# A two-layer decoder trunk on one core: layer normalisation at the mixer joints in two parts, a fourth raw weight buffer, and the first query weights split without a hold

## The chip, the cores and the metric

The kernel runs on one core of one Trainium2 chip. The metric is device time of one execution in microseconds. TensorE (PE in the profile, PEld its weight loads) multiplies, VectorE (DVE) and ScalarE (ACT) do the elementwise work, GpSimd (POOL) a little of it, and SyncE (SP) issues the transfers.

## What is computed

Two layers, each a token mixer, a layer norm, an expert mixer (PEER), a second layer norm and a gated add. Layer 0's mixer is a state-space block (SSD), layer 1's is causal attention (MoBA). 256 tokens, model width 1024, all in float32:

```python
for i in range(DEPTH):
    mix = ssd_mixer(...) if kind == 0 else moba_attention(...)
    x = layer_norm(alpha * x + mix, ln_mix_g[i], ln_mix_b[i])
    ffn = peer_ffn(x, peer_w_q[i], peer_sub_keys[i], peer_u[i], peer_v[i])
    x = layer_norm(alpha * x + ffn, ln_ffn_g[i], ln_ffn_b[i])
    gate = jax.nn.sigmoid((x @ ple_w_gate[i]).astype(jnp.float32)).astype(x.dtype)
    x = x + gate * (p[i] @ ple_w_proj[i])
```

`layer_norm` takes mean and variance of a token's 1024 values, scales by `rsqrt(var + eps)`, then by `g`, and adds `b`. `peer_ffn` makes queries `xb @ w_q`, scores them against keys, and sums over the chosen ones of 16384 experts (128 chunks `u` on the way in, 128 chunks `v` on the way out; this kernel multiplies with all of them and weights the rest with zero).

## The kernel before

**Weights come in chunks.** A chunk is a [128 x 1024] float32 tile of 512 KB. `chunk` takes one of three `raw` buffers, has SP load it, and `split` makes two halves of each value, in the type fp32r: ScalarE copies the rounded value (`hi`, L113), VectorE subtracts it from the raw one (`lo`, L114). Both go to a tile `hl`, of which there are four. `mm3` then does three matmuls for one float32 product (hi·hi, hi·lo, lo·hi; L138). A raw buffer is free again when `lo` is done. All loads are issued by SP in the order of the program, so a load that waits for a raw buffer holds what is behind it.

**The order on each engine** is not written out by hand: a scheduling layer places the instructions of all engines by its own estimates, and `after(marks)` (a hold) keeps an instruction from being placed ahead of the marked ones. A fourth buffer or another order in the code therefore moves instructions in other places too.

**The stages.** SSD of layer 0 (to about 224 us), then the expert mixer: queries and keys, 128 chunks `u`, 128 chunks `v`. In its tail (`TAIL = 5`) the last five experts are multiplied for the first token half of 128 alone, then for the second, so that the first half's norm can start. Among the last 26 experts before those stand seven chunks `w_pg` of the output gate, so that 33 chunks come where PE has the matmuls of 26. Each layer then ends with norm and gate; layer 1 begins with attention, and repeats the rest.

**The joint** between mixer and expert mixer is `end_mixer`: the last output products of both token halves (`tb` 0 and 1) into four PSUM accumulators `acc`, then `layer_norm` of half 0 with transposes (`turn`) of its result into `xT`, which all queries read; then products `project` of the per-layer input, which need no norm; then `layer_norm` of half 1 and its transposes. `layer_norm` consists of: two sums with the residual on VectorE (L175), two tiny operations (L178, L179), the square on ScalarE (L181), two products of the centred value (L184), the variance (L185), a power on GpSimd (L186), and two scalings (L189).

**The first query chunk** (`hc == 0`) has its `lo` subtracted by GpSimd (`lo_on`), and its split is held behind the square and the power of half 0.

Of the kernel before, what the change touches and what calls it, by code (L numbers as in the profile page):

```python
# [17 lines left out]
P = 128  # L18
T = 256
# [38 lines left out]
class Net:  # L58
# [50 lines left out]
    def raw(self):  # L109
        return self.stream.tile([P, 1024], F32, tag="raw", bufs=3, name=self.name("raw"))  # L110

    def split(self, hi, lo, src, lo_on=None):
        a = self.nc.scalar.copy(hi, src)  # L113
        b = (lo_on or self.nc.vector).tensor_tensor(lo, src, hi.bitcast(F32), op=OP.subtract)  # L114
        return a.ins, b.ins

    def chunk(self, src, w=1024, parts=1, hl=None, lo_on=None, after=()):
        raw = self.raw()
        if hl is None:
            hl = self.stream.tile([P, 2, 1024], F32R, tag="hl", bufs=4, name=self.name("hl"))  # L120
        n = w // parts
        for k in range(parts):
            r = slice(k * n, (k + 1) * n)
            dma = self.nc.sync.dma_start(raw[:, r], src[:, r])
            with self.after(after):
                hi, lo = self.split(hl[:, 0, r], hl[:, 1, r], raw[:, r], lo_on)
            self.pace.marks = (dma.ins, hi) if lo_on else (dma.ins, hi, lo)
        return hl
# [40 lines left out]

    def layer_norm(self, tb, acc, x, gb, junks, dump, pool, keep=None, turns=True):  # L170
        nc = self.nc
        sm = pool.tile([P, 6], F32, tag="ln_s", bufs=2, name=self.name("ln_s"))
        for h in range(2):
            v = x[:, tb, h * 512:(h + 1) * 512]
            nc.vector.scalar_tensor_tensor(v, v, ALPHA, acc[h], op0=OP.mult, op1=OP.add, accum_out=sm[:, h:h + 1])  # L175
        v = x[:, tb, :]
        mean, neg, var = sm[:, 2:3], sm[:, 3:4], sm[:, 4:5]
        nc.vector.tensor_scalar(neg, sm[:, 0:1], sm[:, 1:2], -1.0 / D, op0=OP.add, op1=OP.mult)  # L178
        nc.vector.tensor_scalar(mean, sm[:, 0:1], sm[:, 1:2], 1.0 / D, op0=OP.add, op1=OP.mult)  # L179
        junk = junks[:, tb]  # L180
# [25 lines left out]
    def end_mixer(self, i, accs, x, gb, dump, pool, last, lhs):  # L206
# [20 lines left out]
        self.norm_marks[1] = self.norm_marks[1][:2] + (last,)  # L227

# [429 lines left out]
    def peer(self, i):  # L658
        nc, dram = self.nc, self.dram
        with self.tc.tile_pool(name=f"peer{i}", bufs=1) as pool:  # L660
# [251 lines left out]
            self.layer_norm(1, accs[1], x, gb0, gb1, junk[:, 0, 0], pool, turns=False)  # L912

# [129 lines left out]
```

## Time and profile before

| what | value |
|---|---|
| median of 3 runs | 2028.8 us (2027.66 to 2029.06) |
| the profiled execution, its own time | 2027.79 us |
| its span, first to last instruction | 2026.0 us |
| PE busy / PEld busy | 2001.7 us (99%) / 1817.5 us (90%) |
| DVE / ACT / POOL busy | 1553.3 (77%) / 1010.6 (50%) / 26.4 us (1%) |
| read from HBM | 360.92 MB, 181 GB/s over the span |
| granted clock of TensorE | 1.000 over the span |

A busy share close to one does not say that PE is at its peak: matmuls overlap, and their ends are modelled. The count of matmuls in a stretch of given length says more, and so does what PE waited for. The queues in the profile are `q1 hardware_dynamic` (all loads) and two for instructions; there is none that GpSimd's software would feed.

### The profile page before, as it was taken

To read this page: it belongs to the slowest core of one execution; us is meant where nothing else is said; L and a number is where in the kernel's file an instruction comes from. 1 tells how busy PE (TensorE), PEld (TensorE's weight loads), DVE (VectorE), ACT (ScalarE), POOL (GpSimd) and SP (SyncE) were. 2 spreads that over 40 slices of the span, in tenths; PEclk is the share of its full clock that TensorE was granted. 3 is DMA by queue.
4 is the path that set the end of the run, shared out by engine and by line. 5 is a ranking of instruction groups with operands and counts; after the bars stand their busy time and mean duration, and the time that the engine had idled before them with its cause. 6 is when DMAs were issued, how large, how long until landed. Compare 5 with 4: busy or idle time off the path is not lost.

```text
span 2026.0 us, 36796 instructions
## 1 busy us (share of the span) xinstructions
PE 2001.7 (99%) x14706; PEld 1817.5 (90%) x14706; DVE 1553.3 (77%) x3050; ACT 1010.6 (50%) x1472; POOL 26.4 (1%) x31
## 2 busy tenths in 40 slices
PE   9999999999999999999999999999999999999998
PEld 8888899999999888888879889999999988888887
DVE  8786659997777988866665655999787888986665
ACT  6754544455444444445545654445544444445553
POOL 0001000000000000000000000000000000000000
PEclk9999999999999999999999999999999999999999
DMA  7446655555555555666745555555555555566672
GB/s 270 156 133 197 210 174 181 179 184 184 159 173 161 176 167 187 226 209 201 235 138 177 177 179 165 186 179 187 175 161 175 159 178 175 178 214 221 201 227 83
DMA packets 102732, 369.64 MB, mean 182 GB/s; under 512 B 11392, under 2 KB 12320, under 8 KB 100896
## 3 DMA queue, kind: packets, MB, share of 16 engines
q1 hardware_dynamic: 102560, 367.29, 56.1%
q8 instruction: 115, 1.88, 0.4%
q14 instruction: 57, 0.47, 0.1%
HBM read 360.92 MB, written 6.32 MB: 181 GB/s over the span
## 4 chain that ended last, share of the span: by engine, by line
PE 79%; issue 8%; DMA 5%; DVE 5%; ACT 2%; POOL 1%; SPq 0%; POOLq 0%; ACTq 0%
PE mm L138 42%; PE acc L138 31%; DMA raw<-in_v 3%; PE aux L830 3%; DVE hl L114 2%; ACT hl L113 1%; DVE cv_y L351 1%; DMA raw<-in_w_pg 1%; PE aux L689 1%; PE aux L456 0%; DMA raw<-in_w_xbc 0%; PE mm L166 0%; PE mm L371 0%; DMA raw<-in_w_q 0%; POOL sq L477 0%
## 5 line engine op out<-in xcount | busy, mean ns | idle before, releaser
L138 PE MATMUL mm<-xT,hl 128*128 128x256 f32 x8112 | 1003.4, 284 | 1.8 <-DVE hl L114 1.1
L138 PEld LDWEIGHTS mm<-xT,hl 128*128 128x128 f32 x8112 | 981.5, 192 | 6.3 <-issue 2.0
L114 DVE TENSOR_TENSOR hl<-raw,hl 128x1024 fp32r<-128x1024 f32 x624 | 758.6, 1221 | 282.3 <-ACT hl L113 280.2
L113 ACT CAST hl<-raw 128x1024 fp32r<-128x1024 f32 x626 | 654.8, 1047 | 291.6 <-PE mm L138 174.2
L138 PE MATMUL acc<-hl,w 128*128 128x512 f32 x3024 | 697.5, 391 | 1.5 <-DVE hl L114 0.7
L138 PEld LDWEIGHTS acc<-hl,w 128*128 128x128 f32 x3024 | 564.7, 188 | 120.7 <-DVE hl L114 2.3
L113 ACT CAST w<-act 128x256 fp32r<-128x256 f32 x252 | 101.9, 406 | 269.0 <-PE acc L138 261.1
L803 ACT ACTIVATE act<-mm 128x512 f32<-128x512 f32 x128 | 76.5, 598 | 227.6 <-PE mm L138 227.4
L114 DVE TENSOR_TENSOR w<-act,w 128x256 fp32r<-128x256 f32 x252 | 106.0, 421 | 43.7 <-ACT w L113 42.9
L837 DVE SCALAR_TENSOR_TENSOR act<-aux,act 128x256 f32<-128x256 f32 x256 | 90.5, 416 | 26.0 <-PE aux L830 26.0
L821 DVE TENSOR_TENSOR a<-oh,r 128x512 f16<-128x512 f16 x256 | 96.3, 417 | 0.0
L815 DVE TENSOR_TENSOR oh<-iota,r 128x1024 f16<-128x1024 f16 x128 | 87.2, 682 | 0.0
L830 PEld LDWEIGHTS <-oh 128*128 128x128 f16 x2048 | 63.3, 98 | 9.7 <-issue 8.4
L830 PE MATMUL aux<-a,oh 128*128 128x64 f16 x2048 | 70.9, 193 | 0.0
L817 DVE TENSOR_TENSOR oh<-iota,r 128x512 f16<-128x512 f16 x128 | 53.3, 417 | 0.0
L138 PE MATMUL acc<-hl,nhl 128*128 128x512 f32 x192 | 49.2, 407 | 0.0
L138 PEld LDWEIGHTS acc<-hl,nhl 128*128 128x128 f32 x192 | 34.8, 188 | 9.8 <-issue 1.0
L138 PE MATMUL acc<-act,xT 128*128 128x512 f32 (+1 forms) x186 | 40.8, 373 | 0.0
L138 PEld LDWEIGHTS acc<-act,xT 128*128 128x128 f32 x186 | 32.2, 189 | 5.6
L351 DVE SCALAR_TENSOR_TENSOR cv_y<-cv_raw,params,cv_y 128x253 f32<-128x253 f32 (+2 forms) x72 | 34.4, 486 | 2.3 <-ACT cv_y L348 1.8
L727 DVE MAX8 act<-act 128x8 f32<-128x128 f32 (+1 forms) x96 | 32.1, 334 | 2.3
L114 DVE TENSOR_TENSOR act<-raw,act 128x1024 fp32r<-128x1024 f32 x16 | 19.6, 1226 | 16.3 <-ACT act L113 16.2
(213 smaller groups left out, 1048.7 us busy)
## 6 DMA issues: line engine op xcount, KB each, us to landing
raw<-in_u SPq DMA_DIRECT2D x256, 512.0 KB, 3.6
raw<-in_v SPq DMA_DIRECT2D x256, 512.0 KB, 4.3
raw<-in_w_q SPq DMA_DIRECT2D x32, 512.0 KB, 4.5
raw<-in_w_xbc SPq DMA_DIRECT2D x24, 512.0 KB, 3.7
raw<-in_w_z SPq DMA_DIRECT2D x16, 512.0 KB, 3.5
raw<-in_w_so SPq DMA_DIRECT2D x16, 512.0 KB, 4.4
raw<-in_w_pg SPq DMA_DIRECT2D x16, 512.0 KB, 4.5
raw<-in_w_qk SPq DMA_DIRECT2D x16, 512.0 KB, 3.9
```

The source lines that it names most:

```text
L113: a = self.nc.scalar.copy(hi, src)
L114: b = (lo_on or self.nc.vector).tensor_tensor(lo, src, hi.bitcast(F32), op=OP.subtract)
L138: self.nc.tensor.matmul(out, lhs(a), rhs(b), start=start and i == 0, stop=stop and i == 2)
L351: nc.vector.scalar_tensor_tensor(y[:, d:], raw[:, :T - d], w(k), y[:, d:], op0=OP.mult, op1=OP.add)
L689: nc.tensor.matmul(pss[:, tb], q[:, tb * P:(tb + 1) * P], keys[:, hc, :], start=True, stop=True)
L727: nc.vector.max(vals[:, 8:], src)
L803: nc.scalar.activation(act[e // 32][:, e % 32 - 1:e % 32 + 1, :], cur["ph"], AF.Gelu_apprx_tanh)
L815: nc.vector.tensor_tensor(pairs(oh2), every(self.iota, P), twins(i2T, P), op=OP.is_equal)
L817: nc.vector.tensor_tensor(pairs(oh1), every(self.iota[:, 64 * half:64 * half + 64], 64), twins(i1T, 64), op=OP.is_equal)
L821: nc.vector.tensor_tensor(pairs(a2[:, k]), pairs(oh1), twins(g2[:, k], 64), op=OP.mult)
L830: nc.tensor.matmul(pg[:, t, :], oh2[:, t], a2[:, k, t], start=k == 0, stop=k == 1)
L837: nc.vector.scalar_tensor_tensor(v, pg[:, :, 32 * a:32 * a + 32].rearrange("p t e -> p e t"), 2.0 ** -12, v, op0=OP.mult, op1=OP.mult)
```

## The change

1. `raw` has four buffers in place of three, and the program is built with `dynamic_dma_scratch_size=4096`.
2. `layer_norm` is cut into `ln_sums` (residual sums, the two tiny operations, the square) and `ln_scale` (the rest). `end_mixer` calls `ln_sums` for both halves, then `ln_scale` for half 0; `ln_scale` of half 1 stays where its `layer_norm` was. At the joint behind the expert mixer the two parts follow each other as before.
3. The first query chunk is split like all others: `hi` by ScalarE, `lo` by VectorE, with no hold.
4. `norm_marks` loses the power, which no hold needs any more.

```diff
     def raw(self):
-        return self.stream.tile([P, 1024], F32, tag="raw", bufs=3, name=self.name("raw"))
+        return self.stream.tile([P, 1024], F32, tag="raw", bufs=4, name=self.name("raw"))
...
-    def split(self, hi, lo, src, lo_on=None):
+    def split(self, hi, lo, src):
         a = self.nc.scalar.copy(hi, src)
-        b = (lo_on or self.nc.vector).tensor_tensor(lo, src, hi.bitcast(F32), op=OP.subtract)
+        b = self.nc.vector.tensor_tensor(lo, src, hi.bitcast(F32), op=OP.subtract)
...
-    def layer_norm(self, tb, acc, x, gb, junks, dump, pool, keep=None, turns=True):
+    def ln_sums(self, tb, acc, x, dump, pool):
         nc = self.nc
         sm = pool.tile([P, 6], F32, tag="ln_s", bufs=2, name=self.name("ln_s"))
         for h in range(2):
             v = x[:, tb, h * 512:(h + 1) * 512]
             nc.vector.scalar_tensor_tensor(v, v, ALPHA, acc[h], op0=OP.mult, op1=OP.add, accum_out=sm[:, h:h + 1])
-        v = x[:, tb, :]
         mean, neg, var = sm[:, 2:3], sm[:, 3:4], sm[:, 4:5]
         nc.vector.tensor_scalar(neg, sm[:, 0:1], sm[:, 1:2], -1.0 / D, op0=OP.add, op1=OP.mult)
         nc.vector.tensor_scalar(mean, sm[:, 0:1], sm[:, 1:2], 1.0 / D, op0=OP.add, op1=OP.mult)
+        square = nc.scalar.activation(dump, x[:, tb, :], AF.Square, bias=neg, accum_out=var).ins
+        return mean, var, square
+
+    def ln_scale(self, tb, sums, x, gb, junks, keep=None, turns=True):
+        nc = self.nc
+        mean, var, square = sums
         junk = junks[:, tb]
-        square = nc.scalar.activation(dump, v, AF.Square, bias=neg, accum_out=var).ins
...
-        power = nc.gpsimd.tensor_tensor(var, var, self.mhalf[:, :1], op=OP.pow).ins
+        nc.gpsimd.tensor_tensor(var, var, self.mhalf[:, :1], op=OP.pow)
...
-        self.layer_norm(0, accs[0], x, gb, junks, dump, pool, self.x_d[i])
+        sums = [self.ln_sums(tb, accs[tb], x, dump, pool) for tb in range(2)]
+        self.ln_scale(0, sums[0], x, gb, junks, self.x_d[i])
...
-        self.layer_norm(1, accs[1], x, gb, junks, dump, pool, self.x_d[i], turns=False)
+        self.ln_scale(1, sums[1], x, gb, junks, self.x_d[i], turns=False)
...
-                marks = (sq0, pow0) if hc == 0 else (sq0, last) if hc < 2 else (sq1, last) if hc < 4 else ()
-                lo_on = nc.gpsimd if hc == 0 else None
-                self.stationary(pq[:, :T], self.chunk(dram["w_q"][i, hc], lo_on=lo_on, after=marks))
+                marks = () if hc == 0 else (sq0, last) if hc < 2 else (sq1, last) if hc < 4 else ()
+                self.stationary(pq[:, :T], self.chunk(dram["w_q"][i, hc], after=marks))
...
-    nc = bacc.Bacc("TRN2", target_bir_lowering=False, num_devices=1)
+    nc = bacc.Bacc("TRN2", target_bir_lowering=False, num_devices=1, dynamic_dma_scratch_size=4096)
```

What the change does to the order on the engines is seen best at three places. The first is VectorE at the joint of layer 0. `ln_s_2289` are the statistics of half 0, `ln_s_2344` those of half 1 (`ln_s_2295` in the changed kernel), `hl_2390` is the first query chunk, `acc_921` and `acc_922` are half 1's accumulators. Before:

```order
L185 TENSOR_SCALAR ln_s_2289<-ln_s_2289 128x1
L189 SCALAR_TENSOR_TENSOR xn<-junks,ln_s_2289,gb 128x512 x2
L175 SCALAR_TENSOR_TENSOR xn,ln_s_2344<-xn,acc_921 128x512
L175 SCALAR_TENSOR_TENSOR xn,ln_s_2344<-xn,acc_922 128x512
L178 TENSOR_SCALAR ln_s_2344<-ln_s_2344 128x1
L179 TENSOR_SCALAR ln_s_2344<-ln_s_2344 128x1
L114 TENSOR_TENSOR xT<-mm_2300,xT 128x4x128
L114 TENSOR_TENSOR xT<-mm_2309,xT 128x4x128
```

and in the changed kernel, where lines from L176 on have other numbers (the scalings are L193):

```order
L189 TENSOR_SCALAR ln_s_2289<-ln_s_2289 128x1
L193 SCALAR_TENSOR_TENSOR xn<-junks,ln_s_2289,gb 128x512 x2
L114 TENSOR_TENSOR hl_2390<-raw_2389,hl_2390 128x1024
L175 SCALAR_TENSOR_TENSOR xn,ln_s_2295<-xn,acc_921 128x512
L175 SCALAR_TENSOR_TENSOR xn,ln_s_2295<-xn,acc_922 128x512
L114 TENSOR_TENSOR xT<-mm_2306,xT 128x4x128
L177 TENSOR_SCALAR ln_s_2295<-ln_s_2295 128x1
L178 TENSOR_SCALAR ln_s_2295<-ln_s_2295 128x1
```

The sums of half 1 have stayed behind the scalings of half 0, and the subtraction of the first query chunk, which GpSimd did, now stands between the two.

The second place is VectorE at the joint of layer 1 (half 0 is `ln_s_12787`, half 1 `ln_s_12842`, then `ln_s_12793`; `hl_12888` is the first query chunk, `at_12650` the last attention output). Before:

```order
L114 TENSOR_TENSOR at_12650<-aux_12713,at_12650 128x256
L175 SCALAR_TENSOR_TENSOR x,ln_s_12787<-x,acc_11789 128x512
L175 SCALAR_TENSOR_TENSOR x,ln_s_12787<-x,acc_11790 128x512
L178 TENSOR_SCALAR ln_s_12787<-ln_s_12787 128x1
L179 TENSOR_SCALAR ln_s_12787<-ln_s_12787 128x1
L175 SCALAR_TENSOR_TENSOR x,ln_s_12842<-x,acc_11791 128x512
L184 SCALAR_TENSOR_TENSOR junks<-x,ln_s_12787,gb 128x512 x2
L185 TENSOR_SCALAR ln_s_12787<-ln_s_12787 128x1
L175 SCALAR_TENSOR_TENSOR x,ln_s_12842<-x,acc_11792 128x512
L189 SCALAR_TENSOR_TENSOR x<-junks,ln_s_12787,gb 128x512 x2
L178 TENSOR_SCALAR ln_s_12842<-ln_s_12842 128x1
L179 TENSOR_SCALAR ln_s_12842<-ln_s_12842 128x1
```

and in the changed kernel:

```order
L114 TENSOR_TENSOR hl_12888<-raw_12887,hl_12888 128x1024
L114 TENSOR_TENSOR at_12650<-aux_12713,at_12650 128x256
...
L188 SCALAR_TENSOR_TENSOR junks<-x,ln_s_12787,gb 128x512
L175 SCALAR_TENSOR_TENSOR x,ln_s_12793<-x,acc_11791 128x512
L188 SCALAR_TENSOR_TENSOR junks<-x,ln_s_12787,gb 128x512
L175 SCALAR_TENSOR_TENSOR x,ln_s_12793<-x,acc_11792 128x512
L189 TENSOR_SCALAR ln_s_12787<-ln_s_12787 128x1
L177 TENSOR_SCALAR ln_s_12793<-ln_s_12793 128x1
L178 TENSOR_SCALAR ln_s_12793<-ln_s_12793 128x1
L193 SCALAR_TENSOR_TENSOR x<-junks,ln_s_12787,gb 128x512 x2
```

Here the statistics of half 1 have moved ahead of the scalings of half 0, the variance of half 0 has moved behind the last sum of half 1, and the query chunk's subtraction stands ahead of the whole joint.

The third place is TensorE in the SSD stage, where z chunks are multiplied in plain float32 (`mm_671` to `mm_794`, each from a raw buffer of its own), `aux_759` and `aux_764` are small products of the scan, and `aux_811` needs a copy by ScalarE. Before:

```order
L138 MATMUL mm_623<-xT,hl_619 128x256 x24
L416 MATMUL aux_759<-cf_126,bf_125 128x128 x2
L427 MATMUL aux_764<-ident,xs_127 128x128 x4
L371 MATMUL mm_671<-xT_78,raw_672 128x256 x8
L371 MATMUL mm_691<-xT_78,raw_692 128x256 x8
...
L138 MATMUL mm_818<-xT,hl_820 128x256 x11
L441 MATMUL aux_811<-xe_771,bn_809 128x512
L138 MATMUL mm_818<-xT,hl_820 128x256 x13
```

and in the changed kernel:

```order
L138 MATMUL mm_623<-xT,hl_619 128x256 x24
L379 MATMUL mm_671<-xT_78,raw_672 128x256 x8
L424 MATMUL aux_759<-cf_126,bf_125 128x128 x2
L379 MATMUL mm_691<-xT_78,raw_692 128x256 x8
...
L138 MATMUL mm_818<-xT,hl_820 128x256 x22
L449 MATMUL aux_811<-xe_771,bn_809 128x512
L138 MATMUL mm_818<-xT,hl_820 128x256 x2
```

The first plain z product has moved ahead of the scan's products, and on SP its load ahead of the four 1 MB loads of `ac`; `aux_811` has moved 11 matmuls back. Between the joints, in the expert mixers, the order on TensorE is the same in both kernels, and on SP, ScalarE and VectorE only a few neighbours are exchanged.

## Rows read from the trace of the kernel before

**Rows 1.** The page, busy time of each engine with share and count.

```profile
PE 2001.7 (99%) x14706; PEld 1817.5 (90%) x14706; DVE 1553.3 (77%) x3050; ACT 1010.6 (50%) x1472; POOL 26.4 (1%) x31
```

**Rows 2.** Windows: us, busy PE, PEld, DVE, ACT, POOL (count), PEclk, DMA share, GB/s.

```profile
0.00:50.00 50.00, 45.15 (x328) 40.39 (x329) 40.75 (x106) 34.64 (x63) 0.20 (x4) 1.00 0.77 273
900.00:945.00 45.00, 45.00 (x200) 37.25 (x200) 27.35 (x34) 22.31 (x34) 0.00 (x0) 1.00 0.61 194
1000.00:1024.00 24.00, 22.42 (x94) 17.06 (x93) 15.29 (x18) 12.63 (x17) 0.00 (x0) 1.00 0.81 237
1930.00:1960.00 30.00, 29.30 (x128) 23.67 (x127) 18.54 (x22) 16.98 (x24) 0.00 (x0) 1.00 0.72 225
1960.00:1990.00 30.00, 28.38 (x120) 21.84 (x119) 19.43 (x24) 15.44 (x22) 0.00 (x0) 1.00 0.72 227
```

**Rows 3.** Groups by line, 1905 to 1990: busy us, mean ns, idle before, releaser.

```profile
L114 DVE TENSOR_TENSOR hl<-raw,hl 128x1024 fp32r<-128x1024 f32 x29 | 35.5, 1224 | 20.6 <-ACT hl L113 20.6
L113 ACT CAST hl<-raw 128x1024 fp32r<-128x1024 f32 x28 | 29.4, 1050 | 22.9 <-DMA raw<-in_v 22.8
```

**Rows 4.** DMA issues from 1910 to 1987: count, KB each, median us to landing.

```profile
raw<-in_v SPq DMA_DIRECT2D x26, 512.0 KB, 4.4
raw<-in_w_pg SPq DMA_DIRECT2D x7, 512.0 KB, 4.6
```

**Rows 5.** The scalings' line by tile: ns min/median/max, first and last start, forms.

```profile
L189 DVE SCALAR_TENSOR_TENSOR xn<-junks,ln_s,gb x4: 744/750/2861, 212.4 to 221.4; 128x512 f32<-128x512 f32 x4
```

**Rows 6.** Timeline of the joint of layer 0 and the queries behind it.

```profile
212.38 3.53 DVE L189 SCALAR_TENSOR_TENSOR xn<-junks,ln_s,gb 128x512 f32<-128x512 f32 x2 [0.66 <-POOL ln_s L186]
212.44 2.93 POOL L114 TENSOR_TENSOR hl<-raw,hl 128x1024 fp32r<-128x1024 f32 x1
215.83 0.68 DVE L175 SCALAR_TENSOR_TENSOR xn<-xn,acc 128x512 f32<-128x512 f32 x1
215.97 0.66 PE L166 MATMUL mm<-ident,xn 128*128 128x128 f32 x4 [1.52 <-DVE xn L189]
221.64 0.63 PE L166 MATMUL mm<-ident,xn 128*128 128x128 f32 x4 [0.89 <-DVE xn L189]
223.85 11.91 PE L138 MATMUL mm<-xT,hl 128*128 128x256 f32 x96
240.03 1.22 PE L138 MATMUL mm<-xT,hl 128*128 128x256 f32 x8 [0.26 <-DVE hl L114]
```

**Rows 7.** Timeline of the joint of layer 1.

```profile
1178.70 3.51 DVE L189 SCALAR_TENSOR_TENSOR x<-junks,ln_s,gb 128x512 f32<-128x512 f32 x2
1181.60 1.31 PE L166 MATMUL mm<-ident,x 128*128 128x128 f32 x8 [1.84 <-DVE x L189]
1182.13 0.20 DVE L178 TENSOR_SCALAR ln_s<-ln_s 128x1 f32<-128x1 f32 x1
1183.91 1.16 ACT L181 ACTIVATE dump<-x,ln_s 128x1024 f32<-128x1024 f32 x1
1186.90 1.29 PE L166 MATMUL mm<-ident,x 128*128 128x128 f32 x8 [0.99 <-DVE x L189]
1188.93 11.29 PE L138 MATMUL mm<-xT,hl 128*128 128x256 f32 x92 [0.74 <-DVE xT L114]
```

**Rows 8.** Waits of PE from 9 to 205: us in total, times, longest.

```profile
PE aux L495 <- DVE dg L489: 2.5, 2, 1.6
PE mm L138 <- DVE hl L114: 0.8, 2, 0.6
PE mm L371 <- DMA raw<-in_w_z: 0.5, 1, 0.5
```

**Rows 9.** Timeline of the SSD stage: TensorE's plain z products.

```profile
48.64 7.14 PE L371 MATMUL mm<-xT,raw 128*128 128x256 f32 x32 [0.45 <-DMA raw<-in_w_z]
```

**Rows 10.** Groups by line, whole span: the exponentials of the SSD stage.

```profile
L402 ACT ACTIVATE ac<-ac 128x2048 f32<-128x2048 f32 x4 | 7.6, 1904 | 0.0
L401 ACT ACTIVATE ce<-ce 128x1024 f32<-128x1024 f32 x4 | 4.2, 1050 | 0.0
```

More of the change, by code (lines that the diff above doesn't have):

```diff
@@ L109, in raw, with chunk @@
     def raw(self):
-        return self.stream.tile([P, 1024], F32, tag="raw", bufs=3, name=self.name("raw"))
-    def split(self, hi, lo, src, lo_on=None):
+        return self.stream.tile([P, 1024], F32, tag="raw", bufs=4, name=self.name("raw"))
+    def split(self, hi, lo, src):
         a = self.nc.scalar.copy(hi, src)
-        b = (lo_on or self.nc.vector).tensor_tensor(lo, src, hi.bitcast(F32), op=OP.subtract)
+        b = self.nc.vector.tensor_tensor(lo, src, hi.bitcast(F32), op=OP.subtract)
         return a.ins, b.ins
-    def chunk(self, src, w=1024, parts=1, hl=None, lo_on=None, after=()):
+    def chunk(self, src, w=1024, parts=1, hl=None, after=()):
         raw = self.raw()
@@ L125, in chunk @@
             with self.after(after):
-                hi, lo = self.split(hl[:, 0, r], hl[:, 1, r], raw[:, r], lo_on)
-            self.pace.marks = (dma.ins, hi) if lo_on else (dma.ins, hi, lo)
+                hi, lo = self.split(hl[:, 0, r], hl[:, 1, r], raw[:, r])
+            self.pace.marks = (dma.ins, hi, lo)
         return hl
@@ L193, in layer_norm @@
                 nc.sync.dma_start(keep[:, tb, c], x[:, tb, c])
-        self.norm_marks[tb] = (square, power, last)
+        self.norm_marks[tb] = (square, last)
+    def layer_norm(self, tb, acc, x, gb, junks, dump, pool):
+        self.ln_scale(tb, self.ln_sums(tb, acc, x, dump, pool), x, gb, junks, turns=False)
     def ple_load(self, i, pool):
@@ L226, in end_mixer @@
         last = self.turn(x, 1, 1)
-        self.norm_marks[1] = self.norm_marks[1][:2] + (last,)
+        self.norm_marks[1] = self.norm_marks[1][:1] + (last,)
     def ssd(self):
@@ L520, in value_head @@
         acc = [self.acc() for _ in range(2)]
-        hls = [self.chunk(self.dram["w_v"][kp], after=self.norm_marks[1][::2]) for kp in range(4)]
+        hls = [self.chunk(self.dram["w_v"][kp], after=self.norm_marks[1]) for kp in range(4)]
         for kp in range(4):
@@ L673, in query @@
                 pq = self.mm()
-                (sq0, pow0, _), (sq1, _, last) = self.norm_marks[0], self.norm_marks[1]
-                marks = (sq0, pow0) if hc == 0 else (sq0, last) if hc < 2 else (sq1, last) if hc < 4 else ()
-                lo_on = nc.gpsimd if hc == 0 else None
-                self.stationary(pq[:, :T], self.chunk(dram["w_q"][i, hc], lo_on=lo_on, after=marks))
+                (sq0, _), (sq1, last) = self.norm_marks[0], self.norm_marks[1]
+                marks = () if hc == 0 else (sq0, last) if hc < 2 else (sq1, last) if hc < 4 else ()
+                self.stationary(pq[:, :T], self.chunk(dram["w_q"][i, hc], after=marks))
                 if hc < 4:
@@ L904, in peer @@
                 expert_out(e, w, hl, 0)
-            self.layer_norm(0, accs[0], x, gb0, gb1, junk[:, 0, 0], pool, turns=False)
+            self.layer_norm(0, accs[0], x, gb0, gb1, junk[:, 0, 0], pool)
             for n in ORDER[12 - TAIL:]:
-                pgw[divmod(n, 4)] = self.chunk(dram["w_pg"][i, n], after=(self.norm_marks[0][2],))
+                pgw[divmod(n, 4)] = self.chunk(dram["w_pg"][i, n], after=(self.norm_marks[0][1],))
             for e, w, hl in end:
@@ L911, in peer @@
                     self.turn(x, 0, TURNS.index(e))
[L912 removed]
+            self.layer_norm(1, accs[1], x, gb0, gb1, junk[:, 0, 0], pool)
             def project(pg, tb, h, kps, c=slice(0, 512)):
```

## The prediction

> **What bounds the kernel now.** I read the busy shares first, then counts of matmuls in windows, then PE's waits at the places that the order touches. PE is busy for 99% of the span [rows 1], so the question is where it does less than it could in its busy time. For the `v` chunks the window from 900 to 945 gives the measure: 200 matmuls in 45.00 us, 0.225 us each, 2.70 us for the 12 of an expert. In the last 24 us of layer 0's tail PE does 94, which are worth 94 × 0.225 = 21.15 us: 2.85 us are lost. In layer 1's tail 128 in 30 us are worth 28.8 and 120 are worth 27.0: 1.2 and 3.0 lost [rows 2]. The two tails together lose 7.05 us. The two joints lose what PE waits for `xT` there: 1.52 + 0.89 = 2.41 us in layer 0 [rows 6] and 1.84 + 0.99 + 0.74 = 3.57 us in layer 1 [rows 7]. The SSD stage has waits of 3.8 us in its three longest kinds [rows 8]. The granted clock is 1.00 (the level of 2.4 GHz) in each of these windows [rows 2], so it plays no part.
>
> What ends last in the tails is the raw buffer. ScalarE stands idle for 22.9 us ahead of the `hi` copies there, 22.8 of them until a load has landed, and VectorE for ScalarE [rows 3]. A raw buffer goes round in 4.45 us from issue to landing [rows 4] + 1.05 `hi` + 1.22 `lo` [rows 3] and some 0.1 between them = 6.8 us; three buffers give a chunk every 2.27 us. Measured are 33 chunks in the 77 us of that window, 2.33 us each [rows 4]. PE wants 33 chunks in the time of 26 experts, 26 × 2.70 / 33 = 2.13 us each. So the stock in the four `hl` runs down by 0.2 us a chunk, is empty near the end, and there PE waits, most of all when the last five experts are taken for half 0 alone, at 1.35 us a chunk.
>
> **The tails: −6.4 us.** Four buffers at 6.8 us give a chunk every 1.70 us. The DMA engines would then have to bring 524 KB in 2.13 us, 246 GB/s; the start of the kernel has 273 GB/s at a share of 0.77 [rows 2], which is a chunk in 1.92 us. Both are under 2.13, so the stock stays full to the last five. These want five chunks at 1.35 us: four lie ready or in raw buffers, and the fifth goes to a tile of its own and need not wait for an `hl`. I leave 0.6 us for what isn't smooth, and take 7.05 − 0.6 = 6.4. Upper end of the gain: all 7.05. Lower end: the DMA engines stop at the 237 GB/s that they have at the share of 0.81, the highest shown [rows 2], which is 2.21 us a chunk. The shortfall falls from 33 × 0.20 = 6.6 us to 33 × 0.08 = 2.6 us, against a stock that now covers 6.6 − 4.2 = 2.4 in layer 1; but the burst at the end then finds it empty. I put 3.5 there, half.
>
> The row says that there is room, since the engines' share is 0.72 when PE waits [rows 2]. The Trainium skill, "DMA: Bandwidth & Descriptors", section "Queues, rings and completion order", says that on each DMA engine the descriptors of a queue are taken in the order of its ring. By that a fourth load waits behind the other three, each takes longer to land, and more buffers in flight would bring nothing once the ring always holds work; the sum would then be without the 6.4. The share of 0.72 speaks against an always full ring, and I keep 6.4.
>
> **The joint of layer 0: −1.1 us.** A scaling takes 0.75 us, but one took 2.86 [rows 5]: the pair took 3.53 us beside GpSimd's subtraction of 2.93 us [rows 6]. Without that neighbour the pair takes 2 × 0.75 less their overlap, 1.41: 2.12 us gained. What GpSimd did, VectorE now does between the pair and half 1's sums, for 1.22 us [rows 3]. So these sums start 0.9 us earlier, and some 0.2 more, as in the new order half 0's accumulators end three matmuls sooner less one that has been put in front (2 × 0.225 = 0.45, of which I count half). From half 1's sums at 215.83 to the queries at 223.85 the chain is the same 8.0 us [rows 6], and PE's own work in front of half 1's transposes ends earlier than that chain. The wait of 1.52 for half 0 vanishes, that for half 1 takes part of its place. Bounds: nothing, if the subtraction on VectorE finds its chunk late, and 2.41, if no wait is left.
>
> **The joint of layer 1: −1.4 us.** Here too the pair falls from 3.51 [rows 7] to 1.41, 2.10 us. But the variance of half 0 now stands behind half 1's last sum (0.68, as in [rows 6]) and the two tiny operations (some 0.3), so the pair starts 1.0 us later and ends 1.1 earlier. Behind it the two tiny operations are gone, 0.3 more, and half 1's square, which ScalarE began at 1183.91 [rows 7], is done before it is wanted. All that follows moves by 1.4: queries at 1187.5 in place of 1188.93. The query chunk's subtraction stands where VectorE waits for attention's last output and costs nothing there; if its load were late, ScalarE's copy for it would hold the last attention copies behind it. Bounds: nothing, and 3.57.
>
> **The queries: −0.3 us.** One more `w_q` chunk is loaded ahead of the joint, which covers the wait of 0.26 at 240 [rows 6]. Bounds 0 and 0.6.
>
> **SSD: −1.2 us, the least certain.** The first plain z load goes ahead of the broadcast loads of `ac`, so the wait of 0.5 for it goes, and earlier raws should take half or more of the 0.8 for `hl` [rows 8]. The longest, 2.5 for `dg`, I leave as it is: its product has lost a cover of three matmuls (0.36 us) and the chain ahead of it one convolution step. The exponentials, which ScalarE does among the z copies, come a little later, behind one more 512 KB load (1.92 us at 273 GB/s). In the new order a z copy stands behind one pair of them (1.05 + 1.90 us [rows 10]), while PE takes 7.14 us for two z chunks [rows 9], 3.57 for each: it is the slower one, and covers this delay about once. Bounds: a gain of all 3.8 us, and a loss of 1.9.
>
> **Attention, the `u` stage and the even part of `v`: nothing.** Their order on PE is unchanged or nearly so, and in the `v` window no matmul is lost [rows 2]. Earlier loads find no wait there to remove; attention may move by 0.5 either way.
>
> **Sum.** 6.4 + 1.1 + 1.4 + 0.3 + 1.2 = 10.4 us. The profiled execution's own time is 2027.79 us, which gives 2017.4; it lies 1.0 below the median of the runs, and from that the sum is 2018.4. I take 2018.0 us.
>
> **The rivals.**
> - *The tails give nothing back.* Either the DMA engines are full, as by the ring rule above, or the fourth buffer waits for an `hl` and not for a load. For it: a share of 0.81 in the worst stretch. Against it: ScalarE waits for landings in all of the tail and for no `hl` [rows 3]. Time: 2018.0 + 6.4 = 2024.4.
> - *The joints give nothing back*, because half 1's chain, with the subtraction now on VectorE, ends as late as before. For it: 1.22 of the 2.12 us goes back at once. Against it: GpSimd's 2.93 on the same work. Time: 2018.0 + 2.5 = 2020.5.
> - *SSD's waits nearly all go*, since loads come earlier in all of it: 3.8 in place of 1.2, 2015.4.
> - *Slower.* ScalarE's exponentials come to stand in front of PE's z products: PSUM has two buffers for these, so a z copy that waits for a pair of exponentials holds PE. All four pairs are 4.2 + 7.6 = 11.8 us [rows 10]. Time: 2018.0 + 1.2 + 11.8 = 2031.0. It decides once the `ac` loads land later than about 3.57 − 2.95 = 0.6 us per chunk beyond what PE's own z work covers, over all four pairs. Against it: in this trace PE waits 0.5 us for the z load and for no exponential above that [rows 8].
>
> **How the numbers follow.** A measurement of this kernel tells about 0.2%, 4 us, from no change, so faster means under 2024.7 and slower over 2032.9. Chances: the forecast 0.63, no gain in the tails 0.15, none in the joints 0.12, SSD's waits gone 0.06, the exponentials 0.04. The forecast, the joints' and SSD's case are faster, and half of the tails' case, as it lies at the bound: 0.63 + 0.12 + 0.06 + 0.07 = 0.88. The rest of the tails' case and most of the exponentials' is the same; slower needs more than one of these and gets 0.03. The range: the terms' bounds reach from about 2011 (17.4 us of gain) to 2027 (1.6) when all go one way, which they won't; 2013.5 to 2024.0 leaves out more than half of the tails' case, the exponentials' and a little on the low side, together some 0.18.
>
> **What would show it.** In the changed trace, windows at the two tails' ends should hold matmuls at 0.225 us each with no loss over 0.5, and ScalarE should wait there less for landings, at more than 230 GB/s. Both scalings of half 0 should take 0.75 each, GpSimd should have no subtraction, and the queries should begin 1.1 and 1.4 us sooner after the last mixer product than now. Wrong it would be if loads take 6 us or more to land in the tails while chunks still come every 2.3, or if PE waits for a ScalarE copy in the z products.

## The result, and the profile after

The changed kernel takes 2012.58 us (median of 6 runs, 2012.11 to 2014.34) against 2028.23 (6 runs, 2026.55 to 2029.35): ratio 0.9924, 95% interval [0.9913, 0.9935]. It is faster, by 15.7 us where 10.4 were forecast, and lies 0.9 us below the range. A second comparison on another chip (below) gave 2012.74 against 2026.46, 13.7 us.

The profiled execution took 2012.46 us, its span is 2010.3. First the busy times of the page, to be read against [rows 1]:

```profile
PE 1994.8 (99%) x14706; PEld 1818.2 (90%) x14706; DVE 1554.8 (77%) x3052; ACT 1001.0 (50%) x1472; POOL 19.6 (1%) x29
```

PE has the same 14,706 matmuls as before. So the n-th matmul of one trace can be set against the n-th of the other, and the difference of their starts, taken where stages begin, gives what each stage is worth (n is taken at 199.1, 223.8, 245, 1040, 1172.5, 1188.9 and 2000 us of the kernel before; differences are rounded):

| stage | forecast | measured |
|---|---|---|
| SSD, to the last mixer products | −1.2 | −2.2 |
| joint of layer 0 | −1.1 | −1.9 |
| queries of layer 0 | −0.3 | −0.7 |
| tail of layer 0 / of layer 1 | −6.4 | −3.0 / −4.5 |
| attention | 0 | −0.7 |
| joint of layer 1 | −1.4 | −2.1 |
| behind the last matmul | 0 | −0.5 |
| sum | −10.4 | −15.7 |

In all other stages the shift is 0.0. Windows over the tails, as in [rows 2] (us, busy PE, PEld, DVE, ACT, POOL, PEclk, DMA share, GB/s):

```profile
995.00:1019.00 24.00, 24.00 (x108) 19.89 (x106) 16.08 (x25) 11.39 (x16) 0.00 (x0) 1.00 0.70 241
1920.00:1950.00 30.00, 30.00 (x134) 24.87 (x133) 21.29 (x25) 17.93 (x26) 0.00 (x0) 1.00 0.75 246
1950.00:1975.00 25.00, 25.00 (x112) 20.72 (x111) 16.35 (x19) 13.65 (x19) 0.00 (x0) 1.00 0.58 193
```

TensorE now does 134 matmuls in 30 us and 112 in 25, 0.224 and 0.223 us each: nothing is lost. Groups by line in the tail of layer 1, as in [rows 3], and the loads there, as in [rows 4]:

```profile
L114 DVE TENSOR_TENSOR hl<-raw,hl 128x1024 fp32r<-128x1024 f32 x29 | 35.5, 1225 | 11.3 <-ACT hl L113 11.1
L113 ACT CAST hl<-raw 128x1024 fp32r<-128x1024 f32 x29 | 30.4, 1049 | 0.0
```

```profile
raw<-in_v SPq DMA_DIRECT2D x26, 512.0 KB, 4.3
raw<-in_w_pg SPq DMA_DIRECT2D x7, 512.0 KB, 4.4
```

ScalarE's 22.9 us of idle time ahead of the `hi` copies are gone, at 246 GB/s, the rate that the forecast asked for, and a load takes no longer to land than with three buffers (4.3 and 4.4 us against 4.4 and 4.6).

The scalings by tile, as in [rows 5], and TensorE's timeline at the two joints, as in [rows 6, 7]:

```profile
L193 DVE SCALAR_TENSOR_TENSOR xn<-junks,ln_s,gb x4: 747/749/753, 209.2 to 217.2; 128x512 f32<-128x512 f32 x4
L193 DVE SCALAR_TENSOR_TENSOR x<-junks,ln_s,gb x4: 746/750/753, 1170.5 to 1176.0; 128x512 f32<-128x512 f32 x4
```

```profile
211.40 1.03 PE L166 MATMUL mm<-ident,xn 128*128 128x128 f32 x8
217.41 0.63 PE L166 MATMUL mm<-ident,xn 128*128 128x128 f32 x4 [0.65 <-DVE xn L193]
219.68 0.51 PE L138 MATMUL mm<-xT,hl 128*128 128x256 f32 x2 [0.28 <-DVE xT L114]
...
1163.67 4.92 PE L138 MATMUL acc<-hl,at 128*128 128x512 f32 x20
1171.32 0.66 PE L166 MATMUL mm<-ident,x 128*128 128x128 f32 x4 [0.20 <-DVE x L193]
1176.21 1.29 PE L166 MATMUL mm<-ident,x 128*128 128x128 f32 x8 [0.81 <-DVE x L193]
1178.23 1.93 PE L138 MATMUL mm<-xT,hl 128*128 128x256 f32 x14 [0.74 <-DVE xT L114]
```

No scaling is held up any more. Of the 2.41 us that TensorE waited at the joint of layer 0, 0.93 are left; of 3.57 in layer 1, 1.75. PE's waits in the SSD stage, as in [rows 8] (from 9 to 203 us):

```profile
PE mm L138 <- ACT hl L113: 1.2, 1, 1.2
PE aux L449 <- ACT bn L447: 1.1, 2, 0.6
PE mm L138 <- DVE hl L114: 0.8, 1, 0.8
PE aux L503 <- DVE dg L497: 0.8, 1, 0.8
```

The wait for `dg` has fallen from 2.5 to 0.8. The 1.2 and 0.8 for `hl`, at 10 and 11 us, cost only 0.3 net, as the products ahead of them end earlier; in a second profile of the same kernel (run 5) neither is there, so they belong to this execution. Why `dg` comes sooner is seen on VectorE, at the operation ahead of GpSimd's power (`rs`). Before, and then after, where an earlier wait stands in the same queue:

```profile
93.73 0.15 DVE L485 TENSOR_SCALAR rs<-aux 128x2 f32<-128x2 f32 x1
```

```profile
85.75 1.00 DVE L359 SCALAR_TENSOR_TENSOR cv_y<-cv_raw,params,cv_y 128x253 f32<-128x253 f32 x2 [1.97 <-ACT cv_y L356]
...
91.21 0.15 DVE L493 TENSOR_SCALAR rs<-aux 128x2 f32<-128x2 f32 x1
```

Its input is ready at about 91 in both, but in the kernel before VectorE comes to it 2.5 us later: subtractions of chunks that landed late stand ahead. In the changed kernel the chunks landed earlier and VectorE even waits for ScalarE at 85.75. The same subtractions stand ahead of `rs` in both orders; one convolution step (0.48 us) has moved behind it.

### The profile page after: what moved, and what is told of

Same layout as the page of the kernel before. It is cut to its first block, busy times and chain, and to the rows that moved or that the text cites. A ratio compares the mean times of both kernels' runs of the same rounds, so it can differ in the third digit from the quotient of the medians.

```text
span 2010.3 us, 36808 instructions
## 1 busy us (share of the span) xinstructions
PE 1994.8 (99%) x14706; PEld 1818.2 (90%) x14706; DVE 1554.8 (77%) x3052; ACT 1001.0 (50%) x1472; POOL 19.6 (1%) x29
## 4 chain that ended last, share of the span: by engine, by line
PE 95%; DVE 2%; ACT 2%; DMA 1%; issue 1%; POOL 0%; SPq 0%; ACTq 0%; POOLq 0%
PE mm L138 47%; PE acc L138 41%; PE aux L837 3%; PE aux L696 1%; PE aux L584 1%; ACT hl L113 1%; PE mm L379 1%; DMA raw<-in_w_xbc 1%; PE aux L464 0%; DVE hl L114 0%; PE mm L166 0%; PE aux L606 0%; DVE cv_y L359 0%; PE aux L465 0%; POOL sq L485 0%
## 5 line engine op out<-in xcount | busy, mean ns | idle before, releaser
L359 DVE SCALAR_TENSOR_TENSOR cv_y<-cv_raw,params,cv_y 128x255 f32<-128x255 f32 (+2 forms) x72 | 33.9, 477 | 5.4 <-ACT cv_y L356 5.1
L690 ACT COPY act<-mm 128x256 f32<-128x256 f32 x32 | 11.9, 372 | 51.3 <-PE mm L138 51.3
```

Of the source, the lines that this page charges most:

```text
L359: nc.vector.scalar_tensor_tensor(y[:, d:], raw[:, :T - d], w(k), y[:, d:], op0=OP.mult, op1=OP.add)
```

## The experiments

The shifts by stage for all runs, worked out like the table above (us against the profiled execution of the kernel before; attention and joint 1 together, here up to 1200 us, so with the first queries behind the joint; "tails" is layer 0 / layer 1), with the ratio of the timed runs:

| run | SSD | joint 0 | queries | tails | attention, joint 1 | end | sum | ratio, interval |
|---|---|---|---|---|---|---|---|---|
| changed, again | −2.6 | −1.9 | −0.7 | −3.0 / −4.5 | −2.8 | −0.5 | −16.0 | 0.9934 [0.992, 0.9947] |
| 1 fourth raw only | −2.0 | −1.0 | −0.6 | −3.0 / −4.5 | −0.1 | 0.0 | −11.2 | 0.9952 [0.9939, 0.9966] |
| 2 without it | 0.6 | −1.1 | −0.7 | −0.3 / −3.5 | −2.4 | −0.5 | −7.7 | 0.9985 [0.9976, 0.9994] |
| 3 query split only | 0.7 | −0.9 | −0.7 | 0.3 / −2.0 | −0.6 | −0.5 | −3.6 | 0.9986 [0.9977, 0.9995] |
| 4 norm split only | 3.1 | 0.4 | −0.5 | −0.1 / −1.7 | 0.8 | 0.0 | 2.0 | 1.0004 [0.9995, 1.0013] |
| 6 without query split | −1.9 | −1.0 | −0.6 | −3.0 / −4.5 | 0.0 | 0.0 | −11.0 | 0.9948 [0.9935, 0.9962] |
| 7 without norm split | −2.0 | −1.8 | −0.7 | −3.0 / −4.5 | −2.8 | −0.5 | −15.3 | 0.9937 [0.9924, 0.9951] |
| 8 five raw | 1.0 | −1.9 | −0.7 | −3.0 / −4.5 | −2.6 | −0.5 | −12.2 | 0.9948 [0.9934, 0.9962] |
| 9 three raw, five `hl` | 0.1 | −2.8 | −0.5 | −0.4 / 0.0 | −3.0 | −0.5 | −7.0 | 0.9977 [0.9967, 0.9986] |
| 10 GpSimd, no hold | −2.4 | −1.0 | −0.6 | −3.0 / −4.5 | −2.8 | 0.0 | −14.4 | 0.9937 [0.992, 0.9953] |
| 11 five `hl` | −2.5 | −2.7 | −0.1 | −3.0 / −4.5 | −2.6 | −0.5 | −16.0 | 0.993 [0.9914, 0.9947] |
| 12 half 1 first | −2.1 | −1.9 | −0.7 | −3.0 / −4.5 | −3.5 | −0.5 | −16.1 | 0.9928 [0.9911, 0.9944] |

**Run 1: the fourth buffer alone**, in the kernel before:

```diff
-        return self.stream.tile([P, 1024], F32, tag="raw", bufs=3, name=self.name("raw"))
+        return self.stream.tile([P, 1024], F32, tag="raw", bufs=4, name=self.name("raw"))
...
-    nc = bacc.Bacc("TRN2", target_bir_lowering=False, num_devices=1)
+    nc = bacc.Bacc("TRN2", target_bir_lowering=False, num_devices=1, dynamic_dma_scratch_size=4096)
```

> The kernel before with the fourth raw buffer (and the smaller scratch that makes room for it) and nothing else. First theory, each part of the change acts where its own wait stood: this one part takes all of the tails (3.0 us in layer 0, 4.5 in layer 1, read from the shift of the same matmul between the two traces), SSD's 2.2 and the 0.5 behind the last matmul; both joints stay, since GpSimd still subtracts beside the scalings (a scaling of 2.8 to 2.9 us in each). Sum 10.2, so 2017.5 to 2018.5 in place of 2028.2, ratio 0.995. Rival, the buffer also feeds the joints and the queries behind them with earlier chunks: the joints shrink by more than 1 us each here too, 2015 or less, ratio 0.9935 or less. Second rival, SSD's gain came with the other parts: 2020, ratio 0.996.

Measured 2016.57 against 2025.59. SSD and the tails are as the first theory has them, to 0.2 us; the wait for `dg` is 0.7. It is wrong on the 0.5 at the end, and the rival is right in part: joint 0 gains 1.0 here already. Attention gains 0.5 too, but the joint behind it gives 0.4 of that back: a scaling there still takes 2.9 us, TensorE waits 2.08 us for it, and just behind that wait its granted clock stands at 0.50, the level of 1.2 GHz, for 3.4 us.

**Run 2: the rest without the fourth buffer**, the changed kernel with `bufs=3`.

> The changed kernel with three raw buffers: the split norm and the first query weights without GpSimd and hold, no fourth buffer. First theory: the joints' 2.0 and 1.9 us are all here, the wait of 0.5 in the queries too, and the tails stay as they were before (7.5 us of lost time), SSD too: gain 4.4, so about 2023.8, ratio 0.998. Rival, the joints need the fourth buffer because the first query chunk's load now competes with the mixer's last chunks for raw buffers: gain under 2 us, 2026.5 or more, ratio over 0.999, with waits of TensorE for a chunk in the last mixer products.

2022.32 against 2025.59. The joints' gain stays, though in layer 0 it is 1.1 and not 2.0; SSD gains nothing, its `dg` wait is 2.5. The tails moved by 0.3 and 3.5 though nothing there had been changed: see the spread below.

**Run 3: the query split alone**, in the kernel before:

```diff
-                marks = (sq0, pow0) if hc == 0 else (sq0, last) if hc < 2 else (sq1, last) if hc < 4 else ()
-                lo_on = nc.gpsimd if hc == 0 else None
+                marks = () if hc == 0 else (sq0, last) if hc < 2 else (sq1, last) if hc < 4 else ()
+                lo_on = None
```

> The kernel before, with the first query chunk split by ScalarE and VectorE and without its hold, and nothing else: the norm is whole, three raw buffers. First theory: what made the joints long was GpSimd's subtraction beside VectorE's scalings. Without it no scaling takes over 1 us, and each joint gains 1 to 2 us: 2 to 4 in all, 2024.2 to 2026.2, ratio 0.9985. Rival, the order of the sums made the gain: scalings of 0.75 us, but TensorE waits for the transposes' input as long as before, and the time is within 1 us of before, ratio 0.9995 to 1.0005.

2023.35 against 2025.59, inside the first theory's 2 to 4 us. All scalings take 0.75; joint 0 gains 0.9, joint 1 2.1 up to the first query, of which 1.5 goes again in the queries behind it: there the granted clock stands at 0.50 for 3.4 us, and 16 matmuls take 3.37 us that take 1.90 in the kernel before.

**Run 4: the norm in two parts alone**, with GpSimd's subtraction and hold.

> The kernel before, with the norm of the joints cut in two parts (sums and square of both halves first), GpSimd's subtraction and hold kept, three raw buffers. First theory: beside GpSimd's subtraction one scaling in each joint still takes 2.8 to 2.9 us, and the earlier sums save only the two tiny operations and a square that is ready: 0 to 0.8 us in all, ratio 0.9997 to 1. Rival, the order makes the gain: 2 us or more, 2026.2 or less, ratio 0.999 or less.

No gain can be told (1.0004), scalings of 2.8 us in both joints, and neither joint is shorter (+0.4, +0.8). The rival is out. The 3.1 in SSD is a 2.4 us wait for a z load (0.5 before) and, right behind it, a granted clock of 0.50 for 3.4 us, which costs another 1.6; the expectation had neither. The clock falls at joint 1 too, and this profiled execution is the slowest of the run's eleven, so the two joints' small losses are not to be put down to the norm.

**Run 5: the changed kernel again**, on the chip of runs 6 to 8.

> The changed kernel once more, beside the runs that follow, so that all stand against the same runs of the kernel before. The part with the fourth buffer alone gave 0.9952, the joints and queries alone 0.9985, together 0.9937 if they add up. First theory, they add up, and the first comparison's 0.9924 is a draw within its interval and the three-buffer kernel's own spread: 0.9930 to 0.9942, about 2013 where before takes 2025.6. Rival, they help each other (the joint gains more once its last chunks come early): 0.9926 or less.

2012.74 against 2026.46: 0.9934, where the first theory has it. The interval reaches down to the rival's 0.9926 as well, so that the parts add up is likely and not shown.

**Runs 6 and 7: without the query split, without the norm split.** Each takes one part of the changed kernel back.

> The changed kernel with the first query chunk as before: GpSimd subtracts, held behind square and power; four buffers and the norm in two parts stay. First theory, GpSimd's subtraction beside the scalings is what the joints lost: a scaling of 2.8 to 2.9 us comes back in both, TensorE waits 2 to 4 us more than in the changed kernel at the two joints, and the time is that of the fourth buffer alone, ratio 0.9945 to 0.9960. Rival, the norm in two parts carries the joints: within 1 us of the changed kernel.

> The changed kernel with the norm whole in each half (sums, square and scaling of half 0, then those of half 1); four buffers and the new query split stay. First theory, the two parts are worth little by themselves: 0 to 1 us slower than the changed kernel, all of it at the joint of layer 1, where the order differs most. Rival, they are half of the joints' gain: 1.5 to 2.5 us slower, with longer waits of TensorE for the transposes of half 1 in both layers.

2015.97 and 2014.09 against the changed kernel's 2012.74. In run 6 a scaling of 2.8 to 2.9 us is back in each joint, and they lose 0.9 and 2.8 us. Some 1 us of the 2.8 is the clock: it falls to 0.50 behind TensorE's wait of 2.29 us for that scaling, and the two executions with a mean granted clock of 0.999, the profiled one among them, took 2016.86 and 2017.0 us, the three with 1.000 took 2015.86 to 2015.97. In run 7 no stage differs from the changed kernel's first profile by more than its two profiles differ among themselves (0.4), and the joints by 0.1: in the traces the split of the norm is worth nothing. The medians are 1.35 us apart, which is less than the 1.6 to 1.8 us that the five executions of either kernel spread over. The scalings' line in run 6, and TensorE's stretches without and with work at joint 1 (columns as in [rows 2]):

```profile
L193 DVE SCALAR_TENSOR_TENSOR xn<-junks,ln_s,gb x4: 744/751/2879, 209.7 to 218.7; 128x512 f32<-128x512 f32 x4
L193 DVE SCALAR_TENSOR_TENSOR x<-junks,ln_s,gb x4: 741/748/2835, 1171.7 to 1179.2; 128x512 f32<-128x512 f32 x4
```

```profile
1172.30:1174.60 2.30, 0.05 (x1) 0.00 (x0) 2.30 (x2) 0.79 (x3) 1.74 (x1) 1.00 0.01 4
1175.80:1179.00 3.20, 3.20 (x10) 2.52 (x9) 2.54 (x6) 2.14 (x4) 0.54 (x1) 0.50 0.98 275
```

**Run 8: a fifth raw buffer**, `bufs=5`.

> The changed kernel with a fifth raw buffer. First theory, the tails are done: TensorE does 0.225 us a matmul there and ScalarE waits for TensorE, not for loads, so a fifth buffer gives nothing there, and elsewhere little: within 1 us of the changed kernel, with TensorE's tails the same to 0.1 us. Rival, SSD and attention, where the fourth gave 2.5 and 0.5, still wait for loads: 1.5 us or more sooner in SSD. Third, more loads in flight make the first ones land later (the first chunk landed at 8.87 in place of 8.58 with the fourth): the start loses another 0.3.

2016.18, slower than the changed kernel by 3.4. The tails are the same, as is all behind SSD. There one new wait, which none of the three had foreseen, costs 2.2 us, as the order there is another once more. Behind it the granted clock falls to 0.50, and 8 matmuls take 3.34 us in place of 1.87, another 1.5. The wait, and the two stretches (columns as in [rows 2]):

```profile
PE acc L138 <- ACT nhl L113: 2.2, 1, 2.2
...
188.00:190.00 2.00, 0.18 (x1) 0.18 (x2) 2.00 (x4) 0.63 (x2) 1.48 (x1) 1.00 0.92 330
191.30:194.60 3.30, 3.30 (x9) 2.52 (x8) 1.05 (x4) 0.81 (x2) 0.00 (x0) 0.50 0.35 128
```

**Run 9: three raw buffers and five `hl`**, in the changed kernel.

> The changed kernel with three raw buffers and five split tiles in place of four and four: the tails' other way out, more stock in place of a higher rate. Theory of the prediction, the rate of three buffers (a chunk in 2.3 us against 2.13 wanted) empties the stock: one more tile adds 2.1 us of stock to each tail, so of the tails' lost time (7.5 us in the kernel before, 3.8 in the run with three buffers and the other parts) at most 2.1 goes in each, ScalarE still waits for landings by tens of us in the tail, and SSD's wait for the diagonal product stays at 2.4 us. Rival, it is any buffer that is short: both tails run at 0.225 us a matmul and the time is that of the changed kernel within 1 us.

2021.85. The rival is out. The theory's bound of 2.1 a tail holds, ScalarE still waits 18.6 us for landings ahead of the `hi` copies, and the wait for `dg` is there with 3.1; but far less than 2.1 is gained: the tails lose nearly all that they lost before (7.0 of 7.5 us), although there is more stock. What TensorE waits for near the end is another thing. ScalarE's timeline there, TensorE's, and the window behind it:

```profile
1976.09 1.04 ACT L113 CAST act<-raw 128x1024 fp32r<-128x1024 f32 x1 [1.67 <-DMA raw<-in_v]
1977.04 0.40 ACT L113 CAST w<-act 128x256 fp32r<-128x256 f32 x1
...
1977.49 0.73 PE L138 MATMUL acc<-hl,w 128*128 128x512 f32 x2 [1.71 <-ACT w L113]
...
1979.50:1982.80 3.30, 3.30 (x10) 2.53 (x9) 0.00 (x0) 0.00 (x0) 0.00 (x0) 0.50 0.00 0
```

ScalarE stands 1.67 us for a load, and behind it in its queue stands the copy of `w`, the other operand of products whose chunk is already there. So a late load does not only draw on the stock; it stops ScalarE, and all that ScalarE has still to do. The same wait stands in the tail of layer 0, 1.5 us. Behind the one of layer 1 (and 0.56 more for `w`) the granted clock falls to 0.50: 8 matmuls take 3.31 us, against 1.81 in the changed kernel, so 1.5 us of this tail's loss is the clock.

**Run 10: GpSimd again, but without the hold**, in the changed kernel.

> The changed kernel, where GpSimd again subtracts the first query chunk but without the hold. In layer 1 its subtraction then stands ahead of the norm's power on GpSimd, so ahead of the joint; in layer 0 it stands behind the power, beside the scalings as before. Theory, what costs is that the subtraction lies beside VectorE's scalings: layer 0 has a scaling of 2.8 to 2.9 us again and loses 0.8 to 1.0 us at its joint, in layer 1 all scalings take 0.75 and the joint is that of the changed kernel within 0.5 us; sum about 1 us slower than the changed kernel. Rival, it is the slow path of the query chunk itself (2.9 us of GpSimd in place of 1.2 of VectorE): both layers lose, 3 us together as in the run with the hold.

2013.77. The theory holds in each layer, the rival in none: layer 0 loses 0.9 us, layer 1 nothing. The scalings by tile:

```profile
L193 DVE SCALAR_TENSOR_TENSOR xn<-junks,ln_s,gb x4: 744/751/2879, 209.1 to 218.2; 128x512 f32<-128x512 f32 x4
L193 DVE SCALAR_TENSOR_TENSOR x<-junks,ln_s,gb x4: 745/750/753, 1171.3 to 1176.8; 128x512 f32<-128x512 f32 x4
```

and in the timeline the pair of scalings of layer 0 and GpSimd's two subtractions:

```profile
209.10 3.55 DVE L193 SCALAR_TENSOR_TENSOR xn<-junks,ln_s,gb 128x512 f32<-128x512 f32 x2 [0.66 <-POOL ln_s L190]
209.16 2.94 POOL L114 TENSOR_TENSOR hl<-raw,hl 128x1024 fp32r<-128x1024 f32 x1
...
1162.93 2.37 POOL L114 TENSOR_TENSOR hl<-raw,hl 128x1024 fp32r<-128x1024 f32 x1 [106.08 <-ACT hl L113]
```

In layer 0 it runs beside the scalings, in layer 1 eight us ahead of them, while VectorE is nearly idle.

**Runs 11 and 12: what could come next.** Run 11 has a fifth `hl`; run 12 takes half 1's centred products, variance and power ahead of half 0's transposes.

```diff
...
-        self.ln_scale(0, sums[0], x, gb, junks, self.x_d[i])
+        self.ln_mid(0, sums[0], x, gb, junks)
+        self.ln_scale(0, sums[0], x, gb, junks, None, turns=False)
+        self.ln_mid(1, sums[1], x, gb, junks)
+        for h in range(2):
+            self.turn(x, 0, h)
...
```

> The changed kernel with a fifth split tile beside its four raw buffers. Theory, TensorE is at its full rate wherever chunks stream, so more room changes nothing there: within 1 us of the changed kernel, ratio 0.9928 to 0.9940. Rival, SSD and attention still wait for split chunks: 1.5 us or more sooner there, ratio under 0.9925.

> The changed kernel with one more step of half 1 moved ahead at the joints: its centred products, variance and power stand ahead of the splits of half 0's transposes on VectorE. Theory, the joint is now bounded by VectorE's chain for half 1, in which a split of half 0 (0.69 us) stands between the two products in layer 1: 0.7 us less from the mixer's last products to the queries in layer 1, 0 to 0.7 in layer 0, together up to 1.4, ratio to before 0.9923 to 0.9932, not to be told from the changed kernel by its time but in the trace. Rival, half 0's splits now end last: the joints are as long as in the changed kernel or longer by up to 0.7.

2012.02 and 2012.00: a little under the changed kernel's two medians, but not to be told from it. In run 12 the way from the last mixer products to the queries of layer 1 is 14.04 us in place of 14.56:

```profile
1163.74 4.92 PE L138 MATMUL acc<-hl,at 128*128 128x512 f32 x20
...
1177.78 2.41 PE L138 MATMUL mm<-xT,hl 128*128 128x256 f32 x18 [1.10 <-DVE xT L114]
```

In layer 0 nothing moved. Run 11 shortens joint 0 by 0.8 and gives 0.5 of it back in the queries.

## Why the prediction was right and wrong

**The tails: right in place and remedy, 6.4 for 7.5.** The fourth buffer takes it all; the fifth adds nothing, the rate wanted is the rate measured. Three things were off. The reserve of 0.6 us "for what isn't smooth" was not needed. The upper end of 7.05 was no upper end: windows that count whole matmuls saw 0.5 us less of the loss than the shift does. And run 9 does not bear out the picture of a stock that runs empty: more stock alone gives 0.5 in its profiled execution, by estimate 2.0 if the 1.5 us of the lower clock are left out. The low end, DMA engines that stop at 237 GB/s, was far off; so was the rival that loads queue up and land later. What the Trainium skill says in "DMA: Bandwidth & Descriptors", section "Queues, rings and completion order", of descriptors taken in the ring's order is not refuted by that: a load in the tail took no longer to land (4.3 and 4.4 us against 4.4 and 4.6), so the ring was not always full.

**Joint 0: 1.1 for 1.9.** The 0.9 from GpSimd is what runs 3, 6 and 10 show. The rest comes with the fourth buffer (1.0 in run 1), not from the norm. In run 1 half 0's last accumulator ends 0.88 us sooner, counted from the last product of `dg` ahead of it. About 0.4 of that are waits of weight loads for `hl` within the mixer's last products, which the prediction had not looked for; the other 0.45 are two matmuls, of which it counted half. A fifth `hl` ends these waits too: run 9, with three raw buffers, gains 2.8 here.

**Joint 1: 1.4 for 2.1, attention 0 for 0.7.** All of the joint's gain is the query split's (runs 6 and 7); the prediction credited 0.3 of it to the norm's two parts, which give nothing. What it had too small was the start of the pair of scalings: from half 0's first sum it is 5.14 us in the changed kernel (1165.37 to 1170.51) and 4.41 before, 0.7 later and not 1.0; and the sums themselves start some 0.3 earlier, as one more of the mixer's last products has moved ahead. Attention gains with the fourth buffer (0.5 to 0.7 in runs 1, 6, 7 and 10, nothing in runs 2 to 4; run 9 has 0.5 with three raw buffers and five `hl`), a little over the 0.5 allowed for. In the profiled executions of runs 1 and 6 the joint behind it gives this back, in a stretch at a granted clock of 0.50.

**SSD: 1.2 for 2.2.** The step that failed is "the longest, 2.5 for `dg`, I leave as it is". With three raw buffers it is 2.4 to 3.1 (runs 2, 3, 4, 9), with four or five 0.7 to 0.8 (the changed kernel, runs 1, 6, 7, 8, 10, 12); only run 11, with a fifth `hl` besides, has 1.4. The prediction looked at what the order did to this product; what counted was how far VectorE's queue was behind. The plain z products waited for no exponential: the slower rival is out.

**Queries: 0.3 for 0.7.** All runs but one gain 0.5 or more here, run 4 too, which has neither an earlier load nor a fourth buffer. So the wait in the profile before belongs to that execution or its order; the reason given for the term is not what the runs show, and that the term has the right sign is luck.

**The range.** No one term was far off, but all were on the same side, and that is the step that failed in the range: the bounds would add up "when all go one way, which they won't". They did, as one cause stood behind most of them: run 1 shows the fourth buffer at work in SSD, joint 0, attention and both tails, which came out 1.0, 0.8, 0.7 and 1.1 us over the forecast, 3.6 of the 5.3 that were missing. To narrow 2011, the sum of the bounds, to 2013.5 was to treat one error as several. The bounds themselves were too near as well: the tails (7.5 for at most 7.05), attention (0.7 for 0.5) and the queries (0.7 for 0.6) passed them, and the 0.5 behind the last matmul had been put at nothing without a look.

**A draw.** Three-buffer kernels spread widely: in runs 2, 3 and 4 the tails lost 1.7 to 3.8 us less than in the profiled execution of before, with nothing changed in them, so that 7.5 is an upper value for what the fourth buffer gives there. On one chip the kernel before ranged from 2022.79 to 2028.54 in 27 runs, run 1 from 2015.61 to 2016.58 in 5. The clock is part of this spread: run 9's executions with a mean granted clock of 1.000 took 2017.23 to 2021.68, those with 0.997 and 0.998 2023.65 to 2025.2. Some 2 us of the 15.7 may thus be the first comparison's own; the second has 13.7, still above the 10.4, but less than the 14.7 from 2028.2 down to the range's 2013.5. So the forecast was too small in both, and that it left the range hangs in part on the draw.

## What to carry to other kernels

Terms that one cause drives are added with one error, not with several that cancel: ask of each bound what would have to be true for it, and whether the next bound needs the same thing. A late load costs more than its consumer's wait, as each engine works in order: look at what stands behind the waiting instruction, on ScalarE (`w` in run 9) and on VectorE (`rs` in SSD). An idle engine's help is not free if the engine that it helps slows down beside it: here 1.2 us of work moved to GpSimd cost VectorE 2.1 us per joint, and in layer 1 moving it eight us ahead did as well as taking it back (run 10). Before a lost stretch is put down to a wait, look at the clock behind the wait: in six of the runs TensorE lost some 1.5 us more by it.

## What had not been expected of the hardware

- GpSimd's subtraction takes 2.37 us with VectorE nearly idle (run 10). Beside the scalings it depends on who begins. In layer 0 of run 10 the first scaling began 0.06 us ahead: GpSimd's subtraction took 2.94, and the second scaling 2.88. In layer 1 of run 6 GpSimd began 0.07 ahead:

```profile
1171.68 2.36 POOL L114 TENSOR_TENSOR hl<-raw,hl 128x1024 fp32r<-128x1024 f32 x1
1171.75 3.50 DVE L193 SCALAR_TENSOR_TENSOR x<-junks,ln_s,gb 128x512 f32<-128x512 f32 x2 [0.35 <-POOL ln_s L190]
```

  It took no longer than alone, and the first scaling 2.84. The Trainium skill, "SBUF — State Buffer", section "Who interferes with whom", calls the port pair that the two share an exclusive lock, which whoever issues first holds for a whole instruction. Both traces agree with it to 0.2 us.
- TensorE's granted clock falls behind some of its waits. In runs 1, 3, 4 (twice), 6, 8 and 9 it stands at 0.50, the level of 1.2 GHz, for 3.3 to 3.5 us, each time at the end of or soon behind a wait: of 1.71 to 2.44 us in all but run 3, which has two, of 0.99 and 0.74. The matmuls of such a stretch take some 1.5 us more than at 1.00. In its profiled execution the kernel before waited 1.84 us at joint 1 and the clock stayed at 1.00; what decides is not shown.
- Loads that are queued together land close behind each other. At the start of the changed kernel ScalarE's copies wait for the first chunks:

```profile
8.89 1.04 ACT L113 CAST hl<-raw 128x1024 fp32r<-128x1024 f32 x1 [1.60 <-DMA raw<-in_w_xbc]
...
10.94 1.05 ACT L113 CAST hl<-raw 128x1024 fp32r<-128x1024 f32 x1 [0.87 <-DMA raw<-in_w_xbc]
12.22 1.05 ACT L113 CAST hl<-raw 128x1024 fp32r<-128x1024 f32 x1 [0.24 <-DMA raw<-in_w_xbc]
```

  The last two are 1.28 us apart, 524 KB in 1.28 us or some 410 GB/s, though single loads take over 4 us to land in the tail. The prediction had reckoned with 1.92 us a chunk, the rate of the first 50 us as a whole.
- Behind the last matmul, all kernels without GpSimd's subtraction end 0.5 us sooner (the changed kernel, runs 2, 3, 7, 8, 9, 11, 12), and none of those with it (before, runs 1, 4, 6, 10). In the traces it is a closing step of GpSimd: from its clearing of the semaphores to the end of the `DRAIN` behind it go 0.55 us in these and 0.07 in the others. Why is open.
